# A decoder layer on one Trainium2 core: attention's probabilities turned by VectorE blocks and transfers through DRAM instead of TensorE transposes

## The chip, the core and the metric

The kernel runs on one core of one Trainium2 chip. The metric is the device time of one execution in microseconds (us). A core has TensorE (PE, matrix products, with a weight load PEld that overlaps them), VectorE (DVE), ScalarE (ACT), GpSimd (POOL) and SyncE (SP). Each engine works through its own instructions in order; semaphores make one engine wait for another. SP's and POOL's queues issue transfers (DMAs).

## What is computed

One layer of a hybrid decoder on 256 positions of 2048 channels, all in float32: a norm, one input projection, a gated DeltaNet branch (GDN, 8 heads of 128), a block-sparse attention branch (MoBA, 8 heads of 128), a merge by sigmoid gates, an output projection, a gated MLP with a short convolution, and a final norm. With 256 positions there is one attention block, so MoBA is plain causal attention:

```python
s_own = jnp.einsum('hqd,hld->hql', qn, k_own)
s_own = jnp.where(own_ok[None], s_own, NEG_INF)
p = jax.nn.softmax(jnp.concatenate([s_past, s_own], axis=-1), axis=-1)
...
return jnp.einsum('hqkl,hqkld->hqd', p_past, v_sel) + jnp.einsum('hql,hld->hqd', p_own, v_own)
```

## The kernel before

Weights come from DRAM in pieces of 1 MB (tile wraw, four buffers, SP's queue). Each is split into a high and a low part: ACT casts the high part wh (L110), DVE subtracts to get the low part wl (L107), each in two halves of 1024 columns and with two buffers. A block of output channels is 48 main matmuls of 256 columns (L100, names ps_...): for each of 16 pieces of the contraction wh times the high and the low part of the activations, then wl times the high part. These main matmuls are nearly all of PE's work.

The stages of the main matmuls in order are: four groups of GDN (three chunks q, k, v and the gate z, ps_gdn and ps_z), four groups of MoBA (two chunks q and k for a pair of heads, ps_moba, and in every other group the values of four heads, ps_v), 16 chunks of gates (ps_gate), the branch projections (ps_br), the output projection (ps_wo), up (ps_up) and down (pd).

Everything small runs in the background of these. `main_mm` counts what it issues, and after every 1700 units (a matmul of 256 columns counts 108, one of 512 counts 215) it calls `tick`, which gives each background generator in the list `bg` one turn. `yield from wait(n)` lets n turns pass, so that a transfer can land while main matmuls run. The generators are `decay` (GDN's decays), `rotary` (cosines and sines of the positions into CS, through DRAM), `gdn` (the recurrence, one for each pair of heads) and `moba` (attention, one for each pair of heads). After the third MoBA group, turns are given without main matmuls until one generator is left, and after the gates until none is.

The order written so is not the last word. The framework's scheduler moves each engine's instructions by its own model of when inputs are ready, so one edit can move rows far away from it. Tiles come from pools. Tiles with one tag share buffers, and a tile must wait until the readers of the tile before it in its buffer are done.

`moba` for one pair of heads, by lines: L667 brings the rotated quarter of q and k into X_ (POOL's queue, four transfers); L669 to L673 rotate on DVE (Xc, Xs); L674 puts it back; L680 and L681 make the scores of one head in PSUM (sc), the rows of the second half of the positions against all keys and those of the first half against the first half; L684 to L693 add the mask nm3 and take the softmax into s_ (DVE, with ACT's Exp at L689 and L690). Then, two turns later, L699 to L701 turn the three blocks of 128x128 of one head on PE into PSUM (pT, keys on the partitions), ACT copies them into pT_ (L703), and L708 and L710 multiply with v into py_b, which ACT copies into yb (L712). sc, pT and py_b use the pool ps_sd of five PSUM banks; py_b is taken before the scores.

Of the kernel before, what the change touches and what calls it, by code (L numbers as in the profile page):

```python
# [39 lines left out]
def const_array():  # L40
# [10 lines left out]
    nm3[:, 1:, :] = np.where(i[None, :] <= i[:, None], 0.0, -1e30)[:, None, :]  # L51
# [21 lines left out]
def layer_kernel(ctx: ExitStack, tc: tile.TileContext, xT, pos, cst, vec, convw, ffw, bdv,  # L73
# [235 lines left out]
    dr = gdn_st.enter_context(tc.tile_pool(name="dr", bufs=2, space=bass.MemoryType.DRAM))  # L309
# [3 lines left out]
    def rotary():  # L313
        posi = m.tile([P, 32], I32, name="posi", tag="pT_")
        sp.dma_start(posi, pos)
        ang = m.tile([P, 32], F32, name="ang", tag="s_")
        dve.tensor_copy(ang, posi)
        dve.tensor_scalar(ang, ang, C["invf"], None, op0=ALU.mult)
        qn = m.tile([P, 32], F32, name="qn", tag="s_")
# [9 lines left out]
        lo1 = m.tile([P, 32], F32, name="lo1", tag="pT_")  # L329
        lo2 = m.tile([P, 32], F32, name="lo2", tag="pT_")  # L330
# [27 lines left out]
        cs = m.tile([P, 2, 32], F32, name="cs_", tag="s_")  # L358
# [11 lines left out]
    def decay():  # L370
        nz, ez, den, sv, s2, pv, spv, gt = (m.tile([16, T], F32, name=n, tag=t) for n, t in (
            ("nz", "qk0"), ("ez", "qk0"), ("den", "qk1"), ("sv", "qk1"), ("s2", "s_"), ("pv", "s_"),
            ("spv", "pT_"), ("gt", "pT_")))
# [25 lines left out]
        rem = m.tile([16, P], F32, name="rem", tag="qk0")  # L399
# [257 lines left out]
    def moba(h0, q, k, v):  # L657
        X_ = m.tile([P, 2, P], F32, name="X_", bufs=1)
        Xc = m.tile([P, 2, P], F32, name="Xc", bufs=1)
        Xs = m.tile([P, 2, P], F32, name="Xs", bufs=1)  # L660
# [15 lines left out]
        py = r3(sdt("py_b"), T)  # L676
        ss = []
        for j in range(2):
            ps = sdt("sc")
            pe.matmul(ps[:, :T], q[:, j, P:], k[:, j, :], start=True, stop=True)  # L680
            pe.matmul(ps[:, T:T + P], q[:, j, :P], k[:, j, :P], start=True, stop=True)  # L681
            s_ = m.tile([P, 3 * P], F32, name="s_")
            ss.append(s_)
            dve.tensor_tensor(s_, ps[:, :3 * P], C["nm3"], op=ALU.add)  # L684
            mx = m.tile([P, 4], F32, name="mx")
            dve.tensor_reduce(mx[:, 0:1], s_[:, :T], axis=AX.X, op=ALU.max)
            dve.tensor_reduce(mx[:, 1:2], s_[:, T:], axis=AX.X, op=ALU.max)
            dve.tensor_scalar(mx[:, 0:2], mx[:, 0:2], -ATT_SCALE, None, op0=ALU.mult)
            act.activation(s_[:, :T], s_[:, :T], AF.Exp, bias=mx[:, 0:1], scale=ATT_SCALE, accum_out=mx[:, 2:3])  # L689
            act.activation(s_[:, T:], s_[:, T:], AF.Exp, bias=mx[:, 1:2], scale=ATT_SCALE, accum_out=mx[:, 3:4])  # L690
            dve.reciprocal(mx[:, 2:4], mx[:, 2:4])
            dve.tensor_scalar(s_[:, :T], s_[:, :T], mx[:, 2:3], None, op0=ALU.mult)
            dve.tensor_scalar(s_[:, T:], s_[:, T:], mx[:, 3:4], None, op0=ALU.mult)  # L693
            yield
        yield from wait(2)
        for j in range(2):
            s_ = ss[j]
            pp = sdt("pT")
            pe.transpose(pp[:, 0:P], s_[:, T:], ident)  # L699
            pe.transpose(pp[:, P:T], s_[:, 0:P], ident)  # L700
            pe.transpose(pp[:, T:T + P], s_[:, P:T], ident)  # L701
            pT = m.tile([P, 3 * P], F32, name="pT_")
            act.copy(pT, pp[:, :3 * P])  # L703
            ss[j] = pT
            yield
        for j in range(2):
            pT = ss[j]
            pe.matmul(py[:, j, :], v[:, 0, j * P:(j + 1) * P], pT[:, :T], start=True, stop=False,  # L708
                      skip_group_check=True)
            pe.matmul(py[:, j, P:], v[:, 1, j * P:(j + 1) * P], pT[:, T:], start=False, stop=True,  # L710
                      skip_group_check=True)
# [253 lines left out]
```

## Time and profile before

| what | value |
|---|---|
| median of the timed runs | 1455.61 us (three: 1451.09 to 1455.78) |
| the profiled execution's own time | 1450.71 us |
| its span, first to last instruction | 1448.9 us |
| granted TensorE clock | 0.998 |
| transfers of weights | 1 MB each, about 4.8 to 5.1 us from issue to landing |
| transpose of one head (L699 to L701), first and last | start 305.2 and 392.7 us |
| products with v (L708), first pair and fourth | start 308.9 and 394.9 us |
| rotary's first load and its last step on DVE | 73.3 and 110.9 us |

The profile is one execution. A row of the timeline has the start, the length, the engine, the line, the operation, the tiles as out<-in, and in square brackets the idle time of the engine before it with what ended it. A matmul's length includes its way through the array; one starts before the one ahead of it has ended, so prices are read from starts. A product of float32 operands stands as two PE rows in the trace, one of the split operands or a transpose as one.

### The profile page before, as it was taken

The numbers are of one execution on the slowest core, as the hardware profiler recorded it, in microseconds if no ns is written. First come the engines' busy times: TensorE is split into PE (matmuls) and PEld (weight loads), VectorE is DVE, ScalarE is ACT, GpSimd is POOL, SyncE is SP. The second block draws the span as 40 slices with busy tenths as digits, with TensorE's granted clock in tenths as the row PEclk, the third lists the DMA queues.
The fourth block names the chain that finished last, engine by engine and source line by source line (L and its number), as shares of the span: only waits on it lengthen the run. The fifth ranks groups of instructions, "written<-read, shape, count | busy, mean of one in ns | idle before, by whom it ended". The sixth has DMA issues, their size and how long they took to land.

```text
span 1448.9 us, 26704 instructions
## 1 busy us (share of the span) xinstructions
PE 1437.9 (99%) x11232; PEld 1381.6 (95%) x11232; DVE 951.5 (66%) x1389; ACT 741.1 (51%) x1052; POOL 158.1 (11%) x237
## 2 busy tenths in 40 slices
PE   9999999999999999999999999999999999999997
PEld 8999999999999999999999999999999998888886
DVE  7889887765654546767776666666666666555454
ACT  5675774446553444444554545445455455444444
POOL 0024133230030000101120000000000000000000
PEclk9999999999999999999999999999999999999999
DMA  9466656545455555566585555555555555555552
GB/s 342 150 204 211 202 183 210 191 162 173 161 196 180 201 195 187 201 213 226 202 268 197 201 183 199 202 182 199 195 188 200 195 187 202 189 189 203 187 191 88
DMA packets 47465, 283.79 MB, mean 196 GB/s; under 512 B 7744, under 2 KB 8912, under 8 KB 15216
## 3 DMA queue, kind: packets, MB, share of 16 engines
q1 hardware_dynamic: 40352, 270.37, 53.7%
q0 software_dynamic: 6272, 9.61, 2.6%
q8 instruction: 88, 1.44, 0.4%
q10 hardware_dynamic: 720, 2.10, 0.4%
q14 instruction: 33, 0.27, 0.1%
HBM read 275.33 MB, written 3.82 MB: 193 GB/s over the span
## 4 chain that ended last, share of the span: by engine, by line
PE 95%; ACT 2%; DMA 1%; DVE 1%; issue 0%; SPq 0%; ACTq 0%
PE ps_up L100 33%; PE pd L88 17%; PE ps_gate L100 12%; PE ps_gdn L100 7%; PE ps_moba L100 6%; PE ps_wo L100 6%; PE ps_br L100 6%; PE ps_v L100 3%; PE ps_z L100 2%; DMA wraw<-in_w_gdn 1%; PE g L88 1%; DVE wl L107 0%; ACT wh L110 0%; PE ps_bd L88 0%; PE po L88 0%
## 5 line engine op out<-in xcount | busy, mean ns | idle before, releaser
L107 DVE TENSOR_TENSOR wl<-wraw,wh 128x1024 fp32r<-128x1024 f32 (+1 forms) x500 | 598.9, 1235 | 185.8 <-ACT wh L110 185.2
L110 ACT CAST wh<-wraw 128x1024 fp32r<-128x1024 f32 (+1 forms) x500 | 496.6, 1041 | 416.0 <-PE ps_up L100 160.4
L100 PE MATMUL ps_up<-h,wh 128*128 128x256 f32 x2816 | 479.3, 276 | 0.0
L100 PEld LDWEIGHTS ps_up<-h,wh 128*128 128x128 f32 x2816 | 424.1, 188 | 0.1
L100 PE MATMUL ps_up<-h,wl 128*128 128x256 f32 x1408 | 388.7, 276 | 0.0
L100 PEld LDWEIGHTS ps_up<-h,wl 128*128 128x128 f32 x1408 | 264.3, 188 | 0.0
L100 PE MATMUL ps_gate<-hc,wh 128*128 128x256 f32 x1024 | 175.7, 277 | 0.0
L100 PEld LDWEIGHTS ps_gate<-hc,wh 128*128 128x128 f32 x1024 | 154.5, 188 | 0.0
L100 PE MATMUL ps_gate<-hc,wl 128*128 128x256 f32 x512 | 141.8, 277 | 0.0
L88 PE MATMUL pd<-wl,ah 128*128 128x512 f32 x336 | 129.5, 389 | 0.0
L88 PE MATMUL pd<-wh,al 128*128 128x512 f32 x336 | 129.1, 389 | 0.0
L100 PE MATMUL ps_gdn<-hc,wh 128*128 128x256 f32 x704 | 124.7, 280 | 0.0
L100 PEld LDWEIGHTS ps_gdn<-hc,wh 128*128 128x128 f32 x704 | 107.3, 188 | 0.3 <-ACT wh L110 0.3
L100 PE MATMUL ps_gdn<-hc,wl 128*128 128x256 f32 x352 | 98.2, 279 | 0.8 <-DVE wl L107 0.8
L100 PEld LDWEIGHTS ps_gate<-hc,wl 128*128 128x128 f32 x512 | 96.1, 188 | 0.1
L100 PE MATMUL ps_moba<-hc,wh 128*128 128x256 f32 x512 | 92.4, 281 | 0.0
L88 PE MATMUL pd<-wh,ah 128*128 128x512 f32 x336 | 92.1, 389 | 0.0
L200 DVE TENSOR_TENSOR unf<-ps_up,R 128x512 f32<-128x512 f32 x44 | 30.4, 692 | 89.2 <-PE ps_up L100 89.2
L100 PE MATMUL ps_wo<-mc,wh 128*128 128x256 f32 x512 | 87.1, 276 | 0.0
L839 POOL TENSOR_TENSOR acts<-sg,cvf 128x256 f32<-128x256 f32 x44 | 32.4, 737 | 439.2 <-ACT sg L838 432.1
L100 PEld LDWEIGHTS ps_moba<-hc,wh 128*128 128x128 f32 x512 | 78.7, 189 | 0.1
L100 PEld LDWEIGHTS ps_wo<-mc,wh 128*128 128x128 f32 x512 | 77.0, 188 | 0.0
(448 smaller groups left out, 1973.0 us busy)
## 6 DMA issues: line engine op xcount, KB each, us to landing
wraw<-in_w_up SPq DMA_DIRECT2D x88, 1024.0 KB, 4.8
wraw<-in_w_dn SPq DMA_DIRECT2D x44, 1024.0 KB, 4.8
wraw<-in_w_gate SPq DMA_DIRECT2D x32, 1024.0 KB, 4.9
wraw<-in_w_gdn SPq DMA_DIRECT2D x30, 1024.0 KB, 5.1
wraw<-in_w_moba SPq DMA_DIRECT2D x16, 1024.0 KB, 5.0
wraw<-in_w_o SPq DMA_DIRECT2D x16, 1024.0 KB, 4.9
wraw<-in_w_mv SPq DMA_DIRECT2D x8, 1024.0 KB, 5.0
wraw<-in_w_ba SPq DMA_DIRECT2D x8, 1024.0 KB, 4.9
```

The lines of the kernel that those rows point to most:

```text
L88: pe.matmul(ps, a, b, start=(start and i == 0), stop=(stop and i == n - 1), **kw)
L100: pe.matmul(ps, a, b, start=start, stop=stop, skip_group_check=True)
L107: return (eng or dve).tensor_tensor(lo, src, hi.bitcast(F32), op=ALU.subtract)
L110: act.copy(hi, src)
L200: dve.tensor_tensor(dst, ps, r, op=ALU.mult)
L839: pool.tensor_tensor(acts[:, c, :], sg, t[:, 1, :], op=ALU.mult)
```

## The change

The transposes on PE, their PSUM tile and ACT's copies go. In their place, for both heads of a pair together:

- The softmax result of the two heads is one tile s2 of 128 x (2 x 384), one buffer. In each head the block of the first half's rows comes first now, so the mask constant and the slices are swapped; the arithmetic is the same.
- One turn after the softmax, DVE's block transpose turns every 32x32 block of s2 within its band of 32 partitions (`dve.transpose` into Zp, 768 columns).
- Four transfers on POOL's queue write the four bands of Zp into a DRAM tile dP, in runs of 32 elements (768 runs each), and a fifth reads dP into pT, 128 partitions of 768 contiguous elements.
- Ten turns later the products with v read pT. py_b is taken there, after the wait, not before the scores.
- To make room, X_, Xc and Xs become slices of one tile X3 with one buffer, and Zp takes the same buffer; s_ and pT_ have one buffer. rotary's small tiles become slices of one tile in X3's buffer, where nothing earlier stands; before, they shared buffers with decay's tiles. decay's tiles move to other tags. The DRAM pool dr now lives as long as the pool m.

The core of the diff:

```diff
-        py = r3(sdt("py_b"), T)
-        ss = []
+        s2 = m.tile([P, 2, 3 * P], F32, name="s_", bufs=1)
         for j in range(2):
             ps = sdt("sc")
...
-        yield from wait(2)
-        for j in range(2):
-            s_ = ss[j]
-            pp = sdt("pT")
-            pe.transpose(pp[:, 0:P], s_[:, T:], ident)
-            pe.transpose(pp[:, P:T], s_[:, 0:P], ident)
-            pe.transpose(pp[:, T:T + P], s_[:, P:T], ident)
-            pT = m.tile([P, 3 * P], F32, name="pT_")
-            act.copy(pT, pp[:, :3 * P])
-            ss[j] = pT
-            yield
+        yield from wait(1)
+        Zp = m.tile([P, 4, 6, 32], F32, name="Zp", tag="X3", bufs=1)
+        dve.transpose(Zp.rearrange("p r x t -> p x r t"), s2.rearrange("p j (b r k) -> p (j b) r k", r=4, k=32))
+        dP = dr.tile([32, 24 * P], F32, name="dP")
+        for r in range(4):
+            pool.dma_start(dram(dP, 32 * r, (24 * P, 32), (P, 24), (1, 32)),
+                           Zp[32 * r:32 * r + 32].rearrange("p r x t -> p (r x) t"))
+        pT = m.tile([P, 2, 3 * P], F32, name="pT_", bufs=1)
+        pool.dma_start(pT.rearrange("p j t -> p (j t)"), dram(dP, 0, (6 * P, 4), (24 * P, 32), (1, 6 * P)))
+        yield from wait(10)
+        py = r3(sdt("py_b"), T)
...
-    dr = gdn_st.enter_context(tc.tile_pool(name="dr", bufs=2, space=bass.MemoryType.DRAM))
+    dr = m_st.enter_context(tc.tile_pool(name="dr", bufs=2, space=bass.MemoryType.DRAM))
...
-        posi = m.tile([P, 32], I32, name="posi", tag="pT_")
+        tmp = r3(m.tile([P, 6 * P], F32, name="angles", tag="X3", bufs=1)[:, :7 * 32], 32)
+        ang, qn, lo1, lo2, cs, posi = tmp[:, 0], tmp[:, 1], tmp[:, 2], tmp[:, 3], tmp[:, 4:6], tmp[:, 6].bitcast(I32)
...
-        X_ = m.tile([P, 2, P], F32, name="X_", bufs=1)
-        Xc = m.tile([P, 2, P], F32, name="Xc", bufs=1)
-        Xs = m.tile([P, 2, P], F32, name="Xs", bufs=1)
+        x3 = m.tile([P, 6 * P], F32, name="X3", tag="X3", bufs=1)
+        X_, Xc, Xs = (r3(x3[:, a * 2 * P:(a + 1) * 2 * P], P) for a in range(3))
```

Three places in the engines' order matter. PE, second pair of heads, before: the two batches of transposes stand among the q and k matmuls of the fourth group (pT_4008 and pT_4030 are the PSUM tiles of the two heads).

```order
L100 MATMUL ps_moba_4187<-hc_77,wh_4253 128x256 x2
L699 MATMUL pT_4008<-ct_198,s__3893 128x128
L700 MATMUL pT_4008<-ct_198,s__3893 128x128
L701 MATMUL pT_4008<-ct_198,s__3893 128x128
L100 MATMUL ps_moba_4187<-hc_77,wl_4254 128x256
L100 MATMUL ps_moba_4187<-hc_77,wh_4253 128x256 x2
L699 MATMUL pT_4030<-ct_198,s__3941 128x128
L700 MATMUL pT_4030<-ct_198,s__3941 128x128
L701 MATMUL pT_4030<-ct_198,s__3941 128x128
```

In the changed program PE has the products with v of the first pair between the scores of the two heads of the second (sc_3871 and sc_3924); the second pair's own products stand 168 main matmuls and eight small ones later, within the first chunk of gates.

```order
L674 MATMUL sc_3871<-qk1_3680,qk0_3515 128x256
L675 MATMUL sc_3871<-qk1_3680,qk0_3515 128x128
L604 MATMUL po_3900<-u_3707,aq0_2994 128x128
L88 MATMUL po_3900<-u_3707,aq0_2994 128x128
L700 MATMUL py_b_3918<-pT__3634,v__3363 128x256
L702 MATMUL py_b_3918<-pT__3634,v__3363 128x128
L700 MATMUL py_b_3918<-pT__3634,v__3363 128x256
L702 MATMUL py_b_3918<-pT__3634,v__3363 128x128
L674 MATMUL sc_3924<-qk1_3680,qk0_3515 128x256
L675 MATMUL sc_3924<-qk1_3680,qk0_3515 128x128
```

The transposes are gone, and the products that used to stand about 30 main matmuls behind them now stand 168 to over 300 behind the scores; for the fourth pair it is 188.

POOL's queue, before, from the end of the fourth GDN recurrence (E, UB) on: the second pair's rotated q and k go back (L674), then the third pair's are fetched (L667).

```order
L551 DMA E_3447<-dE_3444 128x4x32
L554 DMA UB_387<-dE_3444 32x2x32 x8
L674 DMA qk0_3522<-Xc_3732 16x4x128
L674 DMA qk1_3692<-Xc_3732 16x4x128
L674 DMA qk0_3522<-Xc_3732 16x4x128
L674 DMA qk1_3692<-Xc_3732 16x4x128
L667 DMA X__4212<-qk0_3858 64x1x128 x2
```

The same stretch of the changed program:

```order
L547 DMA E_3440<-dE_3437 128x4x32
L550 DMA UB_387<-dE_3437 32x2x32 x8
L693 DMA dP_3629<-Zp_3627 768x1x32 x4
L696 DMA pT__3634<-dP_3629 128x1x768
L662 DMA X3_3714<-qk0_3515 64x1x128 x2
L662 DMA X3_3714<-qk1_3680 64x1x128 x2
L669 DMA qk0_3515<-X3_3714 16x4x128
```

The first pair's writes of dP and the read of pT stand ahead of the second pair's fetch of its rotated quarter, and so it goes on for each pair; the fetch also needs Zp's buffer.

DVE at the start of the program, before, among the weight halves (wl) and the sum of squares for the first norm:

```order
L107 TENSOR_TENSOR wb2_322<-wbd_192,wb2_322 128x16x16
L281 TENSOR_TENSOR sq1_0_309<-sq1_0_309,sq1_2_313 128x1024
L282 TENSOR_TENSOR sq1_0_309<-sq1_0_309 128x512
L107 TENSOR_TENSOR wl_420<-wraw_417,wh_419 128x1024
L283 TENSOR_TENSOR sq1_0_309<-sq1_0_309 128x256
```

And in the changed program:

```order
L107 TENSOR_TENSOR wb2_322<-wbd_192,wb2_322 128x16x16
L317 CAST angles_2768<-angles_2768 128x32
L281 TENSOR_TENSOR sq1_0_309<-sq1_0_309,sq1_2_313 128x1024
L318 TENSOR_SCALAR angles_2768<-angles_2768,ct_198 128x32
L282 TENSOR_TENSOR sq1_0_309<-sq1_0_309 128x512
L322 TENSOR_SCALAR angles_2768<-angles_2768 128x32
L107 TENSOR_TENSOR wl_420<-wraw_417,wh_419 128x1024
```

rotary's small instructions have moved to the front of the program, from behind decay's last steps.

More of the change, by code (lines that the diff above doesn't have):

```diff
@@ L50, in const_array @@
     nm3 = np.zeros((P, 3, P))
-    nm3[:, 1:, :] = np.where(i[None, :] <= i[:, None], 0.0, -1e30)[:, None, :]
+    nm3[:, 0::2, :] = np.where(i[None, :] <= i[:, None], 0.0, -1e30)[:, None, :]
     c["nm3"] = nm3
@@ L675, in moba @@
         yield from wait(3)
-        py = r3(sdt("py_b"), T)
-        ss = []
+        s2 = m.tile([P, 2, 3 * P], F32, name="s_", bufs=1)
         for j in range(2):
             ps = sdt("sc")
[L680 to L683, printed above, removed]
+            pe.matmul(ps[:, P:3 * P], q[:, j, P:], k[:, j, :], start=True, stop=True)
+            pe.matmul(ps[:, :P], q[:, j, :P], k[:, j, :P], start=True, stop=True)
+            s_ = s2[:, j]
@@ L684, in moba @@
             dve.tensor_tensor(s_, ps[:, :3 * P], C["nm3"], op=ALU.add)
             mx = m.tile([P, 4], F32, name="mx")
-            dve.tensor_reduce(mx[:, 0:1], s_[:, :T], axis=AX.X, op=ALU.max)
-            dve.tensor_reduce(mx[:, 1:2], s_[:, T:], axis=AX.X, op=ALU.max)
+            dve.tensor_reduce(mx[:, 0:1], s_[:, P:], axis=AX.X, op=ALU.max)
+            dve.tensor_reduce(mx[:, 1:2], s_[:, :P], axis=AX.X, op=ALU.max)
             dve.tensor_scalar(mx[:, 0:2], mx[:, 0:2], -ATT_SCALE, None, op0=ALU.mult)
-            act.activation(s_[:, :T], s_[:, :T], AF.Exp, bias=mx[:, 0:1], scale=ATT_SCALE, accum_out=mx[:, 2:3])
@@ L690, in moba @@
-            act.activation(s_[:, T:], s_[:, T:], AF.Exp, bias=mx[:, 1:2], scale=ATT_SCALE, accum_out=mx[:, 3:4])
+            act.activation(s_[:, P:], s_[:, P:], AF.Exp, bias=mx[:, 0:1], scale=ATT_SCALE, accum_out=mx[:, 2:3])
+            act.activation(s_[:, :P], s_[:, :P], AF.Exp, bias=mx[:, 1:2], scale=ATT_SCALE, accum_out=mx[:, 3:4])
             dve.reciprocal(mx[:, 2:4], mx[:, 2:4])
-            dve.tensor_scalar(s_[:, :T], s_[:, :T], mx[:, 2:3], None, op0=ALU.mult)
-            dve.tensor_scalar(s_[:, T:], s_[:, T:], mx[:, 3:4], None, op0=ALU.mult)
+            dve.tensor_scalar(s_[:, P:], s_[:, P:], mx[:, 2:3], None, op0=ALU.mult)
@@ L694, in moba @@
+            dve.tensor_scalar(s_[:, :P], s_[:, :P], mx[:, 3:4], None, op0=ALU.mult)
             yield
[L695 to L705 removed]
@@ L706, in moba @@
-        for j in range(2):
-            pT = ss[j]
-            pe.matmul(py[:, j, :], v[:, 0, j * P:(j + 1) * P], pT[:, :T], start=True, stop=False,
+        yield from wait(1)
[5 more added lines that the diff above has]
+                           Zp[32 * r:32 * r + 32].rearrange("p r x t -> p (r x) t"))
@@ L709, in moba @@
+        pT = m.tile([P, 2, 3 * P], F32, name="pT_", bufs=1)
+        pool.dma_start(pT.rearrange("p j t -> p (j t)"), dram(dP, 0, (6 * P, 4), (24 * P, 32), (1, 6 * P)))
+        yield from wait(10)
+        py = r3(sdt("py_b"), T)
+        for j in range(2):
+            pe.matmul(py[:, j, :], v[:, 0, j * P:(j + 1) * P], pT[:, j, :T], start=True, stop=False,
                       skip_group_check=True)
-            pe.matmul(py[:, j, P:], v[:, 1, j * P:(j + 1) * P], pT[:, T:], start=False, stop=True,
+            pe.matmul(py[:, j, P:], v[:, 1, j * P:(j + 1) * P], pT[:, j, T:], start=False, stop=True,
```

11 lines of the change are left out of this document (3 added, 8 removed).

## The prediction

> **What bounds the kernel now.** I read four views, in this order: the page's busy shares and chain shares, TensorE's waits, the chain in order of time, and TensorE's timeline where the changed code runs.
>
> ```profile
> PE 1437.9 (99%) x11232; PEld 1381.6 (95%) x11232; DVE 951.5 (66%) x1389; ACT 741.1 (51%) x1052; POOL 158.1 (11%) x237
> ...
> PE 95%; ACT 2%; DMA 1%; DVE 1%; issue 0%; SPq 0%; ACTq 0%
> ```
>
> TensorE (PE) is busy 99% of the span and is 95% of the chain that ended last. A busy PE could still be waiting inside its pipeline, so the next view lists all that it waited for in the whole run (total, times, longest).
>
> ```profile
> PE ps_z L100 <- DVE wl L107: 1.5, 2, 1.3
> PE warm L232 <- POOL ones L136: 1.0, 1, 1.0
> PE ps_gdn L100 <- DVE wl L107: 0.8, 1, 0.8
> ```
>
> That is 3.3 us in all, and the same view for 110 us onwards has no row. So in the stage that is changed (MoBA, about 290 to 400 us) the time is the sum of what PE issues. The chain gives the price of one main matmul (start, length, what).
>
> ```profile
> 733.29 239.43 PE ps_up L100 x2112
> ```
>
> 239.43 / 2112 = 0.1134 us for each matmul of 256 columns. The profiled execution took 1450.71 us around a span of 1448.9. I make the sum against it and carry the difference over to the median of the runs, 1455.61, which is 4.9 higher; the runs themselves lie between 1451.09 and 1455.78.
>
> **The PE work that goes.** Before, each pair of heads has six transposes on PE (L699 to L701, two heads of three). Two such batches of the second pair, with the main matmuls around them:
>
> ```profile
> 347.20 0.40 PE L100 MATMUL ps_moba<-hc,wh 128*128 128x256 f32 x2
> 347.44 0.28 PE L100 MATMUL ps_moba<-hc,wl 128*128 128x256 f32 x1
> 347.56 0.40 PE L100 MATMUL ps_moba<-hc,wh 128*128 128x256 f32 x2
> 347.80 0.27 PE L699 MATMUL pT<-ct,s__3893 128*128 128x128 f32 x1
> 347.91 0.27 PE L700 MATMUL pT<-ct,s__3893 128*128 128x128 f32 x1
> 348.02 0.27 PE L701 MATMUL pT<-ct,s__3893 128*128 128x128 f32 x1
> 348.05 0.37 PE L100 MATMUL ps_moba<-hc,wl 128*128 128x256 f32 x1
> 348.25 0.40 PE L100 MATMUL ps_moba<-hc,wh 128*128 128x256 f32 x2
> 348.49 0.27 PE L699 MATMUL pT<-ct,s__3941 128*128 128x128 f32 x1
> ```
>
> The lengths overlap, so I count starts. From batch to batch (347.80 to 348.49) are 0.69 us, holding three transposes and three main matmuls. Three main matmuls with none between take 0.36 (347.20 to 347.56). A batch thus costs 0.69 - 0.36 = 0.33 us. Four pairs have eight batches: **-2.6 us**. That a transpose's length reads 0.27 us is no price: 24 x 0.27 would make 6.5. Scores and products with v stay as they were, though the new order puts some products straight behind scores. With the chain's 0.1134 for a main matmul instead of the 0.12 of these rows a batch costs 0.35, and eight of them 2.8: the other end.
>
> **What comes in its place.** ScalarE loses eight PSUM copies; VectorE (DVE) gets four block transposes of 768 columns; GpSimd's queue (POOL) gets 20 transfers.
>
> ```profile
> L703 ACT COPY pT__4012<-pT x1: 464/464/464, 350.4 to 350.4; 128x384 f32<-128x384 f32 x1
> L809 DVE STREAM_TRANSPOSE xt<-xb x7: 706/712/716, 647.8 to 711.5; 128x512 f32<-128x512 f32 x7
> L107 DVE TENSOR_TENSOR wl<-wraw,wh 128x1024 fp32r<-128x1024 f32 (+1 forms) x500 | 598.9, 1235 | 185.8 <-ACT wh L110 185.2
> ```
>
> The copies were 8 x 0.47 = 3.8 us. A block transpose is 0.712 x 768/512 = 1.07 us, so 4.3 us on DVE. Neither engine sets the end here: DVE stood idle 185 us ahead of its weight halves (wl), waiting for ScalarE, which waits for PE. The new row stands ahead of such a half in all pairs but the first, where it is between two. Cost: nothing, as long as one 1.07 us fits in that idle time.
>
> Products with v now wait for pT from a transfer, not for a PSUM copy. The matmul that waits holds up every main matmul behind it on PE, so the question is whether pT lands in time. First the softmax and what is around it, of the second pair before (PE, then DVE):
>
> ```profile
> 339.44 0.60 PE L680 MATMUL sc<-qk,qk 128*128 128x256 f32 x2
> ```
>
> ```profile
> 340.32 0.55 DVE L684 TENSOR_TENSOR s__3941<-sc,ct 128x384 f32<-128x384 f32 x1
> ...
> 345.59 0.28 DVE L693 TENSOR_SCALAR s__3941<-s__3941,mx 128x128 f32<-128x128 f32 x1
> ```
>
> From the second head's scores to its last scaling are 345.87 - 339.44 = 6.4 us; with the block transpose, 7.5. Then four writes to DRAM and one read. No row has these shapes; the nearest are these: POOL's own time for one issue of E (mean ns) and of UB (least, median, most), UB's times to landing, and the median to landing of four others by their line on the transfers:
>
> ```profile
> L551 POOL DMA_DIRECT2D E<-dE x4 | 3.2, 790 | 3.8 <-DMA dE<-X 3.8
> ```
>
> ```profile
> L554 POOL DMA_DIRECT2D UB<-dE x32: 542/542/560, 133.9 to 295.5; - x32
> ...
> DMA to landing us min/median/max: 1.8/4.4/5.7
> ```
>
> ```profile
> Xa<-dC POOLq DMA_DIRECT2D x4, 512.0 KB, 6.0
> ...
> xn<-xt POOLq DMA_DIRECT2D x16, 128.0 KB, 7.4
> gam<-dG POOLq DMA_DIRECT2D x4, 256.0 KB, 4.1
> ...
> E<-dE POOLq DMA_DIRECT2D x4, 64.0 KB, 2.4
> ```
>
> A write has 768 runs of 128 bytes (96 KB). E has 512 such runs, costs POOL 0.79 us and lands in 2.4; I take 0.9 for an issue. The last of four issues starts 2.7 us in, and lands 2.4 (E) to 5.7 us later (the slowest of the UB rows, several in flight): 5.1 to 8.4. The read of 384 KB lies between gam and Xa: 4.1 to 6.0, and 0.3 us for the hand-over. From scores to pT: 7.5 + 5.1 + 0.3 + 4.1 = **17.0** at best, 7.5 + 8.4 + 0.3 + 6.0 = **22.2** at worst. I take 18, since E is the nearest row and little else is in POOL's queue.
>
> The cover is counted in the new order. Between the second head's scores and the products with v stand 168 main matmuls and eight small ones for the second pair, 188 main ones for the fourth. At 0.1134 us that is 19.1 (about 20.9 with the scores' own 0.6 and the small ones) and 21.3 (22.0). The first and third pairs have over 300 main matmuls' worth. So pT is in time by 3 to 4 us at 18, and at worst 1.3 + 0.2 = **1.5 us** late. Taken: 0.
>
> POOL's queue is in order. The next pair's X loads now stand behind the pT read, which waits for the writes. That is 8 to 16 us behind the block transposes, by the same rows. DVE reads X seven weight halves later (first to second pair); a pair of halves is used up in 48 matmuls, 5.4 us, so that is 19 us. Third to fourth pair it is six halves, 16 us: just enough. Cost 0.
>
> **What moves far from there.** The angles have a buffer that nothing used earlier, so rotary's 33 small DVE instructions, which ran at 77 to 111 us, now stand among rows that ran at 27 to 68, and its position load on SP's queue goes ahead of one weight load's issue instead of a later one. The GDN recurrence of the early groups comes some microseconds later on PE; before, PE never stood waiting for it, and it ends well ahead of the gates. The early stretch is the only one with PE waits:
>
> ```profile
> L327 DVE SCALAR_TENSOR_TENSOR ang<-qn,ang x10: 182/184/189, 79.8 to 108.0; 128x32 f32<-128x32 f32 x10
> ```
>
> ```profile
> 50.79 0.89 DVE L419 SCALAR_TENSOR_TENSOR kq<-un,cwv,kq 128x255 f32<-128x255 f32 x2 [1.51 <-ACT kq L417]
> ...
> 53.95 2.34 DVE L107 TENSOR_TENSOR wl<-wraw,wh 128x1024 fp32r<-128x1024 f32 x2
> ```
>
> ```profile
> 55.21 0.39 PE L100 MATMUL ps_z<-hc,wl 128*128 128x256 f32 x1 [1.28 <-DVE wl L107]
> ```
>
> PE waits at 55.21 for that weight half. Nine rotary instructions now stand between R1's reciprocal and it: at 0.18 us, 1.6 us more wait if none is hidden. But DVE idles 1.51 us in that chain for ScalarE, and only one of the nine stands after that idle time. The other end: the 1.5 us of ps_z waits go away. Taken: 0; kept: -1.5 to +1.6.
>
> **The sum**: -2.6 + 0 + 0 = -2.6, so 1448.1 against the profiled 1450.71, and **1453.0** against the median. That is 0.18%, and about 0.3% (4.4 us) is what a measurement of this kernel can tell from no change.
>
> **Rivals.**
>
> *Late pT* (the other side). The point is the products with v of the second and fourth pairs. If each of these transfers lands as late as xn did, 7.4 us with 16 in flight, pT needs 7.5 + 2.7 + 7.4 + 0.3 + 7.4 = 25.3 us against covers of 20.9 and 22.0. PE stands 4.4 + 3.3 = 7.7 us, less 2.6: +5.1, 1460.7. It decides against the change once transfers take over 15 us from block transpose to pT at both places, where my rows give 9.5 to 14.7. For it: 128-byte runs to DRAM, 3072 for each pair, are new here. Against: E's 512 runs landed in 2.4. The Trainium skill, "DMA: Bandwidth & Descriptors", Specifications, says that pieces under 512 B make the DMA do a read-modify-write; no row here separates that from the rest of E's 2.4. Chance 0.12.
>
> *POOL locked out by DVE.* If POOL could not issue while DVE works, each of five issues could wait out a pair of weight halves, 2.34 us: 5 x (0.9 + 2.34) + 2.4 + 4.1 = 22.7 us after the block transpose, against 13.4 and 14.5 left. PE stands 9.3 + 8.2, less 2.6: +14.9, 1470.5. The row of 32 issues speaks against it: 542 to 560 ns, with DVE busy about two thirds of the time. The Trainium skill, "SBUF — State Buffer", "SBUF: two separate sides", has this as the trap that VectorE blocks GpSimd's DMAs: the two share a port, and a VectorE operation that takes it keeps the descriptors from being written, 620 ns becoming 3100. By that rule the time would be this rival's; the trace does not agree. Chance 0.02.
>
> *Early waits go too.* Moving rotary and decay shifts the chain at 55 us, the ps_z waits vanish, and the batches have their higher price: -2.8 - 1.5 = -4.3, 1451.3. That is at the bound, and with the early waits that are too short for the list it is over it, so I count it as faster. For: rotary's DVE work leaves 77 to 111 us. Against: it arrives ahead of the very wait. Chance 0.20.
>
> *No change at all*: PE's time at this place is set by something that the transposes hide, such as the weights, and the gap is refilled: 1455.6. Against it: no PE wait after 110 us, and a weight megabyte lands in 5 us while PE needs 5.4 for it. Chance 0.08.
>
> **The numbers.** My forecast has 0.58. Faster by over 0.3%: the early-waits case, 0.20. Within 0.3%: 0.58 + 0.08 = 0.66. Slower by over 0.3%: 0.12 + 0.02 = 0.14. For the range, the costs run from -4.3 to -2.6 + 1.5 + 1.6 = +0.5: 1451.3 to 1456.1. The runs of before spread over 4.7 us, mostly to the low side, so a low median would be 1451.09 - 2.6 = 1448.5, or 1447 with the early gain. I give 1447 to 1457, which leaves out the two slow rivals.
>
> **What would show it.** Right: no L699 to L701 rows, PE's count 24 lower, still no PE wait after 110 us, pT landing 9 to 15 us after each block transpose, POOL issues of dP near 0.9 us, the MoBA stretch some 2.6 us shorter. Wrong: a PE wait on pT at the products with v (second or fourth pair), a wl wait behind a DVE wait for X or behind a block transpose, a ps_z wait near 55 us that is longer or gone, or dP landings over 8 us.

## The result and the profile after

The changed kernel is slower: 1470.86 us in the median (1467.15 to 1473.93) against 1454.11 before (1451.09 to 1455.78), a ratio of 1.0114 with a 95% interval of 1.0096 to 1.0133. Its profiled execution took 1470.62 us (span 1468.8), 19.9 more than the one of before. The forecast was 1453.0 within 1447 to 1457.

First the page, PE's row and the shares of the chain, to be held against those in the prediction:

```profile
PE 1441.0 (98%) x11208; PEld 1383.6 (94%) x11208; DVE 952.3 (65%) x1393; ACT 739.1 (50%) x1046; POOL 171.2 (12%) x257
...
PE 84%; DMA 5%; DVE 4%; issue 4%; ACT 2%; POOL 1%; SPq 0%; POOLq 0%; DVEq 0%; ACTq 0%
```

PE has its 24 instructions less, and yet it is no longer 95% of the chain: transfers and VectorE stand in it now. The list of PE's waits (total, times, longest), where before only the start and two ps_z rows stood, says where:

```profile
PE ps_gate L100 <- DVE wl L107: 4.7, 1, 4.7
PE py_b L700 <- DMA pT__3984<-dP: 4.0, 1, 4.0
PE w L589 <- DVE vb L586: 3.5, 1, 3.5
PE ps_z L100 <- DVE wl L107: 2.2, 2, 1.4
PE py L558 <- issue: 1.4, 1, 1.4
PE py_b L700 <- DMA pT__4700<-dP: 1.4, 1, 1.4
...
PE w L579 <- ACT UB L569: 0.9, 1, 0.9
```

There are two places. The rows of w and py belong to the GDN recurrence, at 149 to 213 us, in a stage that the change was not meant to touch. The rows of py_b and ps_gate belong to MoBA; these waits begin at 372, 418 and 456 us. The stretches (length, then PE, PEld, DVE, ACT and POOL busy, granted clock, DMA share, GB/s) show the same, and a third thing, in the column behind POOL:

```profile
110.00:200.00 90.00, 85.13 (x714) 84.31 (x714) 72.72 (x160) 53.42 (x89) 23.61 (x41) 0.98 0.56 186
...
345.00:400.00 55.00, 50.98 (x417) 50.27 (x416) 30.95 (x58) 27.91 (x51) 7.63 (x13) 0.97 0.53 165
400.00:450.00 50.00, 45.25 (x371) 44.85 (x370) 27.04 (x40) 22.66 (x31) 11.15 (x18) 0.93 0.60 179
```

The granted clock falls to 0.93 where PE stood. PE's timeline around the wait at 418 us (start, length, line; idle time and releaser in brackets):

```profile
417.82 0.39 PE L100 MATMUL ps_gate<-hc,wh 128*128 128x256 f32 x2
...
423.30 0.58 PE L100 MATMUL ps_gate<-hc,wl 128*128 128x256 f32 x1 [4.75 <-DVE wl L107]
423.68 0.63 PE L100 MATMUL ps_gate<-hc,wh 128*128 128x256 f32 x2
...
424.32 0.63 PE L100 MATMUL ps_gate<-hc,wh 128*128 128x256 f32 x2
...
428.16 0.48 PE L100 MATMUL ps_gate<-hc,wh 128*128 128x256 f32 x2
```

From 423.68 to 424.32 are three matmuls: 0.213 us each, where 0.113 is the rule. It lasts until 428.16, 22 matmuls, so the wait of 4.75 us cost another 2.2. The granted clock of that stretch is half of the full one (columns as above):

```profile
423.30:428.20 4.90, 4.90 (x23) 4.90 (x24) 4.29 (x7) 1.36 (x2) 2.05 (x4) 0.50 0.57 184
```

The Trainium skill, "TensorE: Matmul & The Clock Gate", "What's actually happening", has the rule: after an idle window of about 3.4 us the array gets every second clock pulse, and it takes about as long of steady work to get them all back. The trace agrees: behind the waits of 3.5, 4.0 and 4.7 us stand 10 to 22 such matmuls, behind those up to 1.4 us one at most.

Now the MoBA waits. The landings in the window 300 to 460 us (times issued, KB, median us to landing), first of before:

```profile
wraw<-in_w_gate SPq DMA_DIRECT2D x21, 1024.0 KB, 4.9
wraw<-in_w_moba SPq DMA_DIRECT2D x4, 1024.0 KB, 4.8
```

and of after:

```profile
wraw<-in_w_gate SPq DMA_DIRECT2D x18, 1024.0 KB, 5.8
wraw<-in_w_moba SPq DMA_DIRECT2D x4, 1024.0 KB, 6.7
...
X<-qk POOLq DMA_DIRECT2D x12, 32.0 KB, 9.5
pT__3984<-dP POOLq DMA_DIRECT2D x1, 384.0 KB, 9.0
pT__4413<-dP POOLq DMA_DIRECT2D x1, 384.0 KB, 10.3
pT__4700<-dP POOLq DMA_DIRECT2D x1, 384.0 KB, 10.3
```

The read of pT takes 9 to 10.3 us, not 4.1 to 6.0; the X loads issued behind it land with it; and the weights beside it come later too (all of this window: 6.43 us on average, 10.3 at most, against 4.91 and 5.6), while PE uses one up in 5.4. The third pair shows what that does, on POOL's queue and then on DVE:

```profile
400.25 1.43 POOL L693 DMA_DIRECT2D dP<-Zp  x2 [18.17 <-DVE Zp L690]
...
409.02 0.69 POOL L696 DMA_DIRECT2D pT__4413<-dP  x1 [4.86 <-DMA dP<-Zp]
409.71 2.04 POOL L662 DMA_DIRECT2D X<-qk  x4
```

```profile
398.98 0.98 DVE L690 STREAM_TRANSPOSE Zp<-s__4323 128x768 f32<-128x768 f32 x1
...
408.49 2.36 DVE L107 TENSOR_TENSOR wl<-wraw,wh 128x1024 fp32r<-128x1024 f32 x2 [3.08 <-ACT wh L110]
421.22 0.29 DVE L666 TENSOR_TENSOR X<-X,CS 128x128 f32<-128x128 f32 x1 [10.36 <-issue]
...
422.03 2.35 DVE L107 TENSOR_TENSOR wl<-wraw,wh 128x1024 fp32r<-128x1024 f32 x2
```

DVE stands 10.36 us in front of X, with the weight halves queued behind it; the half at 422.03 is the one that PE waits for at 418 to 423.30. (The row says "issue"; X's loads landed at 421.21.)

The GDN waits begin with the order of the two recurrences. On POOL's queue, before, then after, in the first recurrence:

```profile
133.13 0.79 POOL L551 DMA_DIRECT2D E<-dE  x1 [1.77 <-DMA dE<-X]
...
148.26 0.54 POOL L510 DMA_DIRECT2D Xa<-dC  x1 [0.93 <-DMA dC<-dA]
```

```profile
142.35 0.53 POOL L506 DMA_DIRECT2D Xa<-dC  x1 [2.73 <-DMA dC<-dA]
142.87 0.80 POOL L547 DMA_DIRECT2D E<-dE  x1
```

Xa is the *second* recurrence's 512 KB. It stood well behind the first one's E, and now stands ahead of it. E landed 2.4 us after its issue before; now 7.8, right behind Xa (150.67 and 150.45). E is also issued 9.7 us later than before, and POOL's queue is not all of that: DVE now has rows of the second recurrence (jk, kq) among those of the first, and dX, the first one's earlier transfer, goes out at 128.16 us, 122.46 before. DVE's next step on E starts at 150.69, and PE's py at 151.04 after its 1.4 us wait. The longest of these waits, of w at 178.7 us, ends with vb on DVE, which stands there behind a step that waited 4.9 us for another small transfer, Xr (issued at 175.83).

### The profile page after: what moved, and what is told of

Read it like the earlier page. It is cut to its first block, busy times and chain, and to the rows that moved or that the text cites. A ratio compares the mean times of both kernels' runs of the same rounds, so it can differ in the third digit from the quotient of the medians.

```text
span 1468.8 us, 26675 instructions
## 1 busy us (share of the span) xinstructions
PE 1441.0 (98%) x11208; PEld 1383.6 (94%) x11208; DVE 952.3 (65%) x1393; ACT 739.1 (50%) x1046; POOL 171.2 (12%) x257
## 4 chain that ended last, share of the span: by engine, by line
PE 84%; DMA 5%; DVE 4%; issue 4%; ACT 2%; POOL 1%; SPq 0%; POOLq 0%; DVEq 0%; ACTq 0%
PE ps_up L100 33%; PE pd L88 16%; PE ps_gate L100 9%; PE ps_wo L100 6%; PE ps_br L100 6%; PE ps_moba L100 5%; PE ps_v L100 3%; PE ps_gdn L100 3%; DVE wl L107 2%; DMA dP<-Zp 1%; DMA wraw<-in_w_gdn 1%; DVE kq L415 1%; PE ps_z L100 1%; DMA pT__4700<-dP 1%; DMA pT__3984<-dP 1%
```

## The experiments

The measured ratios are against the kernel before, on the same chip, with 95% intervals. A counting of matmuls in the traces serves all of them: when the n-th one of 256 or 512 columns starts (scores and products with v left out), as a lag in us behind the kernel before (before's own column is the time itself).

```
n     before   after  early_rotary  late_rotary  after_two  two_gdn
1000   136.7   -1.02      -0.42         3.33       -0.33      1.81
1600   215.4    6.93       5.44         3.95        2.97      2.75
2000   278.7    8.23       6.84         3.97        4.28      2.77
2800   401.5    7.40       6.84        -1.29       -0.38     -3.44
3000   424.4   17.16       6.82         1.98        2.89     -0.17
3200   447.0   20.11       6.82         5.70        4.76      1.71
```

From there on no lag changes by more than 0.1. In the changed kernel 8.2 us are lost by the end of GDN, and 11.9 between 279 and 447 us, which is MoBA's share. There late_rotary loses 1.8 and after_two 0.5, and two_gdn gains 1.1. The 4.0 us that late_rotary has lost before come at 135 to 150 us, from PE waits for weight halves (1.8 for wh, 0.8 for wl) and one of 0.4 of the recurrence; two_reads has them too. One trace is one draw, though: late_rotary, small_read and read_on_sp have the same instructions up to 300 us, and their lags there are 3.97, 2.1 and 0.0. So the verdicts go by the medians.

### The GDN order: late_rotary, early_rotary, rotary_only

late_rotary is the changed kernel with one edit, which brings the GDN order of before back, on POOL's queue and on DVE:

```diff
-        tmp = r3(m.tile([P, 6 * P], F32, name="angles", tag="X3", bufs=1)[:, :7 * 32], 32)
+        tmp = r3(m.tile([P, 6 * P], F32, name="angles", tag="s_", bufs=1)[:, :7 * 32], 32)
...
-            ("nz", "qk0"), ("ez", "qk0"), ("den", "qk1"), ("sv", "qk1"), ("s2", "v_"), ("pv", "v_"),
+            ("nz", "qk0"), ("ez", "qk0"), ("den", "qk1"), ("sv", "qk1"), ("s2", "s_"), ("pv", "pT_"),
```

> The changed kernel, except that rotary's small tiles share a buffer with decay's again, so that rotary and the GDN recurrence stand in the old order. Theory 1 (two separate losses: the buffers given to rotary reorder GpSimd's queue in the GDN stage, +8.2 us there; late transfers cost the rest in MoBA): the PE waits between 149 and 215 us go, the ones at about 372, 418 and 455 us stay, time 1470.9 - 8.2 = 1462.7 us. Rival (the GDN delay is only what the new MoBA transfers and the scheduler's answer to them make of it): the waits at 149 to 215 us stay and the time is above 1469 us.

Measured: 1456.88 us, ratio 1.0028 (1.0007 to 1.0049). The waits at 150 to 215 us are gone, as theory 1 has it, but the time falls by more than 8 us, because in MoBA less is lost too. The list of its PE waits has these two for pT and no ps_gate row:

```profile
PE py_b L700 <- DMA pT__4700<-dP: 1.3, 1, 1.3
PE py_b L700 <- DMA pT__3984<-dP: 0.5, 1, 0.5
```

early_rotary goes the other way: the kernel before, its transposes kept, with rotary(), decay(), the tile X3 and the pool dr of the changed one.

```diff
+        tmp = r3(m.tile([P, 6 * P], F32, name="angles", tag="X3", bufs=1)[:, :7 * 32], 32)
...
-            ("nz", "qk0"), ("ez", "qk0"), ("den", "qk1"), ("sv", "qk1"), ("s2", "s_"), ("pv", "s_"),
-            ("spv", "pT_"), ("gt", "pT_")))
+            ("nz", "qk0"), ("ez", "qk0"), ("den", "qk1"), ("sv", "qk1"), ("s2", "v_"), ("pv", "v_"),
+            ("spv", "qk0"), ("gt", "qk0")))
```

> The kernel before with its PE transposes, but with the buffers of the changed kernel for rotary, decay and X (rotary early). Theory 1: PE waits of 1.6, 3.7 and 2 x 1.1 us appear between 149 and 215 us, none at MoBA, time 1454.1 + 8.2 = 1462.3 us. Rival (the loss needs the new MoBA): same as before, 1454 us.

Measured: 1458.59 us, ratio 1.0041 (1.0026 to 1.0055): 6.0 us. Its trace has the waits of the recurrence (1.7, 1.5 and 0.8 us) and none in MoBA. So this loss needs nothing of the new attention. rotary_only keeps decay's tiles where they were before, in early_rotary:

```diff
-            ("nz", "qk0"), ("ez", "qk0"), ("den", "qk1"), ("sv", "qk1"), ("s2", "v_"), ("pv", "v_"),
-            ("spv", "qk0"), ("gt", "qk0")))
+            ("nz", "qk0"), ("ez", "qk0"), ("den", "qk1"), ("sv", "qk1"), ("s2", "s_"), ("pv", "s_"),
+            ("spv", "pT_"), ("gt", "pT_")))
```

> The kernel before with PE transposes; only rotary's tiles get the buffer of their own, decay keeps its old ones. Rotary runs early as in early_rotary, but in GpSimd's queue the first recurrence's E and UB stand ahead of the second one's dA, dC and Xa, as in the kernel before. Theory 1 (the order of that queue costs, Xa's 512 KB ahead of E): no PE wait between 149 and 215 us, same as before, 1454 to 1455 us. Rival (rotary's early instructions on VectorE and its transfers cost): as early_rotary, 1458.6 us.

Measured: 1452.59 us, ratio 0.9993 (0.9981 to 1.0005). Rotary is as early as in early_rotary, and nothing is lost: it is not rotary's work that costs, but decay's tags, which set the order of the two recurrences. How the order costs is read from the traces: the first recurrence's E lands at 138.7 us here and at 150.6 in early_rotary. Of these 11.9 us 5.1 are the slower landing behind Xa on POOL's queue and 6.8 the later issue, in which DVE's order has a part (dX goes out at 123.4 and 128.7). No run moves the order on one of the two alone. Its PE waits after the start:

```profile
PE ps_gdn L100 <- ACT wh L110: 1.9, 1, 1.9
...
PE py L558 <- issue: 0.7, 1, 0.7
```

The ps_z rows at 55 us, which the prediction spoke of, are gone here (lag -2.1 us at the 600th main matmul); a wh wait at 90 us takes it back (+1.7 at the 800th).

### What the transposes are worth: no_turn, no_turn_kick

no_turn is the kernel before with

```diff
-            pp = sdt("pT")
-            pe.transpose(pp[:, 0:P], s_[:, T:], ident)
-            pe.transpose(pp[:, P:T], s_[:, 0:P], ident)
-            pe.transpose(pp[:, T:T + P], s_[:, P:T], ident)
-            pT = m.tile([P, 3 * P], F32, name="pT_")
-            act.copy(pT, pp[:, :3 * P])
+            pT = s_
```

> The kernel before without the 24 PE transposes and the eight copies; the products with v read the unturned probabilities, so the second branch's values are left wrong and only the time counts. The prediction's term: 24 x 0.11 us = 2.6 us less, 1451.5 us. Rivals: the lengths in the trace are the price, 24 x 0.27 = 6.5 us less, 1447.6 us; or something else fills the place, no change, 1454.1 us.

Measured: 1454.18 us, ratio 0.9998 (0.9984 to 1.0013): no change. Without transposes, copies, transfers or waits, nothing is won. The chain in order of time shows why, first of before, then of no_turn (start, length, what):

```profile
398.21 51.03 PE ps_gate L100 x448
449.25 0.28 PE kick L191 x3
```

```profile
394.25 54.65 PE ps_gate L100 x464
448.90 0.28 PE kick L191 x3
```

51.03 / 448 = 0.1139 us, 54.65 / 464 = 0.1178. The same matmuls run 4% slower in no_turn, without a wait and at a granted clock of 1.00, from the last small products at 394 us until the three idle matmuls that the kernel has ahead of its eighth chunk of gates (L191, kick). 464 x 0.0039 = 1.8 us. The counting of matmuls says the same: between the 2000th and the 2800th (401.5 us in the kernel before) no_turn gains 2.2 us, about what the prediction said of the transposes, and by the 3200th (447.0 us) it has lost 1.5 of them again. no_turn_kick puts three more ahead of the fourth chunk:

```diff
-KICKS = {"gate": (7,), "up": (1, 23)}
+KICKS = {"gate": (3, 7), "up": (1, 23)}
```

> no_turn with three idle matmuls more ahead of the fourth chunk of gates. Theory: in no_turn TensorE gave the 2.6 us back because its main matmuls ran at 117.8 ns instead of 113.3 from 393 us to the next such three matmuls at 449 us (465 of them, 2.1 us); the idle matmuls end that phase, so the rows after about 405 us read 113.3 and the profiled time is 1.3 us (less 0.3 for themselves) below no_turn's 1450.2. Rival (the phase comes from the chunk's place in memory or from other engines' traffic): still 117.8 ns up to 449 us, no gain.

Measured: 1453.88 us, ratio 0.9989 (0.9976 to 1.0002); the profiled execution is 0.9 us below no_turn's. Behind the new kick, at 404.17, its chain has

```profile
404.45 43.58 PE ps_gate L100 x384
```

43.58 / 384 = 0.1135: the idle matmuls end the phase, as the theory has it; the rival falls. What starts it is not settled; it begins behind small PE work. So the transposes are worth some 1.6 us at best, and only with the kick; the interval (-0.3 to 3.5 us) does not rule out nothing.

### More turns, no wait, other queues: wait15, late_wait30, no_wait, read_on_sp, zp_with_pt, late_best

```diff
-        yield from wait(10)
+        yield from wait(15)
         py = r3(sdt("py_b"), T)
```

> The changed kernel with 15 turns in place of 10 between the transfers and the products with v (about 9 us more cover). Theory 1: the two PE waits for pT go (4.2 + 1.4 us, and about 2 us of half-rate matmuls behind the first), the wait for a weight half at 418 us behind DVE's wait for X stays near 5 us: 1470.9 - 7.6 = 1463.3 us. Rival (X is what ends last, the wait at 418 us grows by what the others give back): 1469 us or more.

Measured: 1468.49 us, ratio 1.0101 (1.0077 to 1.0125). The expectation failed, for a reason that the order shows: the products stand 159 and 186 main matmuls behind the scores, where 168 and 188 were. Five more turns did not make the scheduler move them back; the waits for pT are 2.0 and 3.4 us. late_wait30 is late_rotary with `wait(30)`, which does move them (250 and 297):

> late_rotary with 30 turns in place of 10, which in the order is 250 main matmuls (second pair) and 297 (fourth) between the second head's scores and the products, in place of 171 and 186. Theory: both pT waits go (0.5 + 1.3 us), none comes: 1456.9 - 1.8 = 1455.1 us. Rival (the one buffer of pT makes the next pair's read wait for products that stand later, a new wait): 1457 us or more.

Measured: 1458.58 us, ratio 1.0025 (1.0010 to 1.0040). The waits for pT are gone, 2.0 us of scores that wait for the rotated q and k and 0.9 for wl stand in their place: nothing is won. no_wait is late_rotary with the products reading s2:

```diff
-            pe.matmul(py[:, j, :], v[:, 0, j * P:(j + 1) * P], pT[:, j, :T], start=True, stop=False,
+            pe.matmul(py[:, j, :], v[:, 0, j * P:(j + 1) * P], s2[:, j, :T], start=True, stop=False,
...
```

> late_rotary with all transfers, but the products with v read the unturned s2, so nothing waits for pT; the second branch's values are wrong and only the time counts. Theory (in late_rotary the loss is PE's wait for pT and the order it brings, not the transfers' traffic): as no_turn, 1454 us or 0.2% below late_rotary. Rival (the traffic slows the weights): as late_rotary, 1456.9 us, with waits for wl or wh in MoBA.

Measured: 1458.73 us, ratio 1.0054 (1.0032 to 1.0075). The theory falls. In the window 300 to 470 us its PE waits are

```profile
PE ps_gate L100 <- DVE wl L107: 6.6, 2, 5.5
PE ps_gate L100 <- ACT wh L110: 3.6, 1, 3.6
```

No row is for pT, and PE stands all the same, behind X (the 5.5) and behind ScalarE, which in this kernel waits for the last read itself. (This profiled execution was the longest of the twelve, 1471.1.) By the median too, nothing is won by dropping the wait for pT.

read_on_sp is late_rotary with `sp.dma_start` in place of `pool.dma_start` for the read of dP:

> late_rotary, but the read of dP is issued on SyncE's queue, in line with the weights. Theory (GpSimd's queue shares the engines with the weights and loses): in line it lands 1.8 us (384 KB at a megabyte in 4.8) after the weight ahead of it, 2 to 6 us after issue instead of 8.5 to 10.8, and the two pT waits go: 1456.9 - 1.8 = 1455.1 us. Rival 1 (its shape makes it slow): landing still 8 us or more. Rival 2: the weights behind it come too late, waits of ScalarE for wraw reach PE, above 1457 us.

Measured: 1461.91 us, ratio 1.0053 (1.0030 to 1.0077), with waits for pT of 3.2 and 1.9 us and one of 1.1 for q and k. The trace has no landing for these reads, so what they took stays open; in line with the weights they are no cure.

zp_with_pt is the changed kernel with

```diff
-        Zp = m.tile([P, 4, 6, 32], F32, name="Zp", tag="X3", bufs=1)
+        Zp = m.tile([P, 4, 6, 32], F32, name="Zp", tag="pT_", bufs=1)
```

> The changed kernel, but Zp takes the buffer of pT, not the one of X, so that the next pair's X loads needn't wait for the writes of Zp and stand ahead of the dP writes or between them and the pT read. Theory: the wait for a weight half at 418 us behind VectorE's wait for X goes, with its half-rate matmuls: 1470.9 - 4.9 - 2.4 = 1463.6 us. Rival (X only takes up time that PE would spend waiting for pT of the fourth pair): that wait grows from 1.4 to 6 or more, 1469 us.

Measured: 1470.75 us, ratio 1.0119 (1.0097 to 1.0141): the rival's side. The wait behind X at 418 us is gone. With X and so the scores earlier, the third pair has 195 main matmuls ahead of its products in the order, where 298 were, and the waits for pT are

```profile
PE py_b L700 <- DMA pT__4413<-dP: 5.6, 1, 5.6
PE py_b L700 <- DMA pT__3984<-dP: 4.8, 1, 4.8
```

late_best joins this edit to late_rotary, with kicks at (1, 4, 7):

> late_rotary, with Zp in the buffer of pT and two more sets of idle matmuls, ahead of the second and fifth chunk of gates, to end slow phases of the main matmuls. Theory: 1456.9 - 1.5 (phases of 117.8 ns) - 1 (waits for X and pT) = 1454.4 us, the kernel before's time and not better, since the transposes are worth 1 to 2 us at most. Rival (the chain to pT is still late at the fourth pair, 180 main matmuls): 1457 us.

Measured: 1467.40 us, ratio 1.0105 (1.0072 to 1.0137). In the order the third pair has 181 main matmuls of cover, 295 in late_rotary, and PE waits 5.6 us for its pT. None of the six wins anything over the kernel that it edits by more than its interval. In late_wait30, no_wait and zp_with_pt a wait is mended at one customer of the transfers, and others come at the rest: pT, X with the scores, the weights.

### The read itself: small_read, small_read_5, after_small, two_reads

small_read is late_rotary with a quarter of the read:

```diff
-        pool.dma_start(pT.rearrange("p j t -> p (j t)"), dram(dP, 0, (6 * P, 4), (24 * P, 32), (1, 6 * P)))
+        pf = pT.rearrange("p j t -> p (j t)")
+        pool.dma_start(pf[:, :192], dram(dP, 0, (6 * P, 4), (24 * P, 32), (1, 192)))
+        act.copy(pf[:, 192:], s2.rearrange("p j t -> p (j t)")[:, 192:])
```

> late_rotary, but the read of dP brings a quarter of the bytes (192 of 768 columns, 96 KB); ScalarE copies unturned probabilities into the rest, so the second branch's values are wrong and only the landing counts. Theory (a transfer of GpSimd's queue lands only when the weight megabyte in flight beside it is done): landing still 5 to 9 us. Rival (the read is long because of its 384 KB): a quarter of 9, about 2.4 to 3.5 us.

Measured: the reads land in 3.8, 4.0, 4.0 and 6.7 us, between the two: less than the theory says, mostly, and more than a quarter of 9. The second landed at 358.68, 1.05 us behind the weight megabyte that was in flight (357.63). No PE wait is left in MoBA. Timed:

> small_read again, timed: late_rotary with a read of 96 KB in place of 384 KB (three quarters of the probabilities are unturned copies, so the second branch's values are wrong). Theory (the MoBA part of the loss comes from the read's bytes: beside a weight megabyte both take twice as long, so pT, X and weights come late together): no PE wait in MoBA and the kernel before's time, 1454 us, ratio 0.998 to 1.001. Rival (the four writes of 3072 runs of 128 bytes are what costs): as late_rotary, ratio 1.003.

Measured: 1453.88 us, ratio 1.0001 (0.9987 to 1.0014). The four writes in 128-byte runs are all there, and nothing is lost. The rival falls. after_small has the same edit in the changed kernel:

> The changed kernel with the same small read (values of the second branch wrong in the same way). Theory: the 10.6 us that the changed kernel loses over early_rotary's 6.0 go, the 6.0 of the GDN order stay: ratio 1.004, 1460 us, no PE wait at 372, 418 and 455 us. Rival (in the early order the transfers fall in a worse place whatever their size): above 1465 us.

Measured: 1456.84 us, ratio 1.0024 (1.0011 to 1.0037), a little below the theory's 1.004, with an interval that overlaps early_rotary's. The trace has the GDN waits, a lag of 6.0 us at the 1600th main matmul, and in MoBA one wait of 1.8 us, of scores for q and k.

two_reads is late_rotary with

```diff
-        pool.dma_start(pT.rearrange("p j t -> p (j t)"), dram(dP, 0, (6 * P, 4), (24 * P, 32), (1, 6 * P)))
-        yield from wait(10)
+        for o in (0, 3 * P):
+            pool.dma_start(pT.rearrange("p j t -> p (j t)")[:, o:o + 3 * P],
+                           dram(dP, o, (6 * P, 4), (24 * P, 32), (1, 3 * P)))
+            yield from wait(2)
+        yield from wait(6)
```

> late_rotary with the read of dP in two transfers of 192 KB, one for each head. Theory (the bytes beside the weights count, not how they are cut): the second lands 8 to 11 us after the first is issued, weights still take over 7 us in some rows, time as late_rotary, 1457 us. Rival (a long transfer is what holds the others up): both land within 6 us, 1454 us.

Measured: 1453.12 us, ratio 0.9990 (0.9975 to 1.0005). My theory was wrong, the rival right in its time: all the bytes are read, in two pieces, and the loss is gone. It has no more cover: 167 and 181 main matmuls stand between scores and products for the second and fourth pair, 172 and 186 in late_rotary. Its landings in 300 to 460 us:

```profile
wraw<-in_w_gate SPq DMA_DIRECT2D x20, 1024.0 KB, 5.2
wraw<-in_w_moba SPq DMA_DIRECT2D x4, 1024.0 KB, 5.2
...
pT__3634<-dP POOLq DMA_DIRECT2D x2, 192.0 KB, 5.5
pT__3985<-dP POOLq DMA_DIRECT2D x2, 192.0 KB, 5.7
pT__4415<-dP POOLq DMA_DIRECT2D x2, 192.0 KB, 5.3
pT__4703<-dP POOLq DMA_DIRECT2D x2, 192.0 KB, 6.2
```

From the first issue to the second landing are 6.4 to 7.5 us (the rival said 6) for the same 384 KB that took 8.5 to 10.8 in late_rotary. The weights of this window take 5.7 us on average and 8.3 at most, in late_rotary 6.1 and 10.8; X lands in 6.0 in the median, there in 8.9. The Trainium skill, "DMA: Bandwidth & Descriptors", "Queues, rings and completion order", says that each transfer engine takes turns between the queues that have work for it, a packet at a time. That fits the read and the weights slowing each other; why two halves do so less than one whole, no run here shows. Being beside a weight is not all of it either: in the kernel before, the four transfers of Xa, 512 KB each, also had weights in flight beside them and landed in 4.4 to 6.6 us.

### Both causes: after_two, two_gdn, two_gdn_kick

after_two has the edit of two_reads in the changed kernel and nothing else.

> The changed kernel with nothing but its read of dP in two transfers of 192 KB (and six turns behind them in place of ten). Theory now (one read of 384 KB holds up the weights, X and pT; two of half its size do so much less; the GDN order costs on its own): the 10.6 us of MoBA go, the 6.0 of GDN stay, ratio 1.004, 1460 us. Rival (the late order was needed for it): above 1465 us.

Measured: 1459.58 us, ratio 1.0041 (1.0026 to 1.0057): as the theory has it. Not all is gone from MoBA: PE waits twice for the second pair's pT, 0.6 us each, and DVE up to 4.4 us for X, which no longer reaches PE. two_gdn then gives decay buffers that restore the GDN order:

```diff
+        sp_, pt_ = (r3(m.tile([16, 6 * P], F32, name=n, tag=n, bufs=1)[:, :2 * T], T) for n in ("s_", "pT_"))
+        s2, pv, spv, gt = sp_[:, 0], sp_[:, 1], pt_[:, 0], pt_[:, 1]
...
```

> after_two with decay's four later tiles put into the buffers of s_ and pT_, so that GpSimd's queue has the GDN recurrence in the order of the kernel before while rotary stays early, as in rotary_only. Theory: both losses gone, ratio 0.999 to 1.000, as two_reads and rotary_only. Rival: 1.004 or more.

Measured: 1452.25 us, ratio 0.9986 (0.9972 to 0.9999). In its list of PE waits nothing stands after 141 us; the largest are

```profile
PE ps_gdn L100 <- ACT wh L110: 1.8, 1, 1.8
...
PE py L559 <- issue: 0.7, 1, 0.7
```

two_gdn_kick is two_gdn with `KICKS = {"gate": (1, 7), "up": (1, 23)}`.

> two_gdn with three idle matmuls ahead of the second chunk of gates. Theory (in two_reads main matmuls ran at 117.8 ns from about 380 to 445 us; the idle matmuls end that, until the fourth pair's scores may bring it back): 1 to 2.5 us less than two_gdn, ratio 0.998, the only version here that would beat both kernels. Rival (the phase returns at once): same as two_gdn.

Measured: 1450.80 us, ratio 0.9980 (0.9967 to 0.9992). It is below both kernels, by 0.2% under the one before; from two_gdn it can't be told by these intervals. In the traces the main matmuls between 385 and 410 us run at 0.1133 us, at 0.1178 in two_gdn. Its profiled execution was the slowest of its twelve (1454.26) and has a wait that two_gdn's lacks, at the fourth pair, whose halves took 8.8 and 8.3 us:

```profile
PE py_b L704 <- DMA pT__4705<-dP: 2.4, 1, 2.4
```

So the halves can be late as well. And the 0.2% are not shown to be the new attention's: the kernel before was not run with more kicks, and its own trace has some 590 main matmuls at 0.1178, 2.6 us (an estimate, 590 x 0.0044).

The causes in one table (ratios):

```
                        GDN order of the change   GDN order of before
PE transposes           1.0041 (early_rotary)     1 (rotary_only 0.9993)
one read of 384 KB      1.0114 (the change)       1.0028 (late_rotary)
two reads of 192 KB     1.0041 (after_two)        0.9986 (two_gdn), 0.9990 (two_reads)
```

## Why the prediction was wrong

**That PE bounds the kernel, and the transposes' 2.6 us.** The reading was right, the size wrong: no_turn won nothing in the end, no_turn_kick 1.6 us. The term counted starts between neighbours and took a main matmul's price for one number. It has two, 0.1134 and 0.1178, and both stood in the rows quoted: "0.36" for three of them is the slow one. What leaves PE can change which holds for hundreds of matmuls behind it.

**ACT's copies, the block transposes, POOL's issues.** Right. A block transpose took 0.97 to 0.98 us (1.07 said), an issue of dP 0.73 (0.9). POOL was not locked out: that rival's time, 1470.5, is the measured one by chance, and its mechanism is not in the trace.

**pT in time, "Taken: 0".** This step failed, at one term. The second pair's chain from the second head's scores (350.98) to the products with v (376.32) took 25.3 us; 17 to 22.2 were said. The softmax and the writes were near their ends (6.4 us to the end of the block transpose, 7.5 said; 6.2 to 8.8 from the first issue to the last landing, 5.1 to 8.4 said). The read was put between gam and Xa by its bytes, 4.1 to 6.0, and took 9.0 to 10.3: this is the term that was mis-sized. Size matters (a quarter of the read landed in 3.8 to 6.7, a half in 4.8 to 9.4), but why 384 KB take longer here than Xa's 512 KB beside weights stays open. The late-pT rival had the chain to the tenth (25.3) and a chance of 0.12; of its 4.4 + 3.3 us 4.0 + 1.4 came. The tenth is luck: it had the writes at 10.1 us and the read at 7.4, and 8.8 and 9.0 came.

**X behind pT on POOL's queue, "just enough. Cost 0".** Failed as well: 8 to 16 us were said from the block transpose, it was 22.2 (398.98 to 421.2), and the 4.7 us at PE were called zero though the margin was nothing. The rows named as a sign of error, a wl wait behind DVE's wait for X, are there word for word.

**A wait's price.** No sum had what follows a long wait: 22 matmuls at half rate after the 4.7 us, 2.2 us more, and 10 after the 4.0 us.

**Rotary and decay moved early, "-1.5 to +1.6 (taken 0)".** Failed: +6.0 us in early_rotary. The step looked at the place where rotary's rows arrived, 55 us, and rotary costs nothing there (rotary_only). "Before, PE never stood waiting for it" was true of the old order alone. What decay's new tags did to the order of the two recurrences, in POOL's queue and on DVE, was in the order to be read and was passed over. The wait at 55 us itself stayed as it was, 1.4 us for 1.3.

**The sum.** 6.0 (GDN order, early_rotary) and 4.1 (one read, in the old order: late_rotary, whose trace has only 1.8 of its 5.8 us in MoBA) are measured apart; together they make 16.6, not 10.1. With the recurrence late the transfers meet the weights elsewhere: from the second pair's first write to the issue of its read are 9.4 us there and the read takes 9.0, 6.2 and 8.5 in late_rotary, and of these two only there X comes so late that PE stands. That it is this meeting was not tried by itself; with the read in two the extra loss is gone as well.

## What to carry to other kernels

Work that is taken off the bounding engine and given to transfers has to be priced beside the transfers already in flight: look at what the weights land in, and leave them their rate; one large read next to them may be worth cutting in two. When an edit gives tiles other buffers, read the order of every in-order queue far from the edit, for large transfers that now stand ahead of small ones that someone waits for. And before work is removed from a full engine, see whether the rest keeps its rate without it.

## What the runs showed of the hardware

- Main matmuls of the same shape run for long stretches in one of two phases, 0.1134 or 0.1178 us, at a granted clock of 1.00 in both. The longer slow phases lasted some 30 to 80 matmuls in the kernel before, and one 464 in no_turn; they can begin behind small matmuls. Three idle matmuls ended one in both places looked at (no_turn at 449 us, no_turn_kick at 404 us), and in the kernel before the second pair's transposes did (0.118 us in front of them at 347 us, 0.1134 behind them from 349.5).
- A read of 384 KB on POOL's queue beside 1 MB weight transfers landed in 8.4 to 12.4 us over all kernels that made it there, its halves in 4.8 to 9.4 each.
- Small transfers of POOL's queue take longer beside a weight: in the kernel before, 12 of dA, dX, dE, E, UB and the rotated q and k that were issued with no weight between its issue and its landing took 2.0 us in the median, 60 that were issued beside one took 3.8.
